# Reciprocal roots of head sums: spread to channel rows through DRAM instead of through TensorE

## The chip, the cores and the metric

The kernel runs on one core of one Trainium2 chip. The metric is the device time of one execution in microseconds (us); the median over the runs counts. One more execution of the same program was recorded by the hardware profiler, and its trace gives the rows that are quoted.

Engines are called as in the profile: PE is TensorE's matrix multiply, PEld its weight load, DVE is VectorE, ACT is ScalarE, POOL is GpSimd, SP is SyncE. "L681" is line 681 of the kernel before. A name with q (SPq) is an engine's DMA-issuing part.

## The reference

One layer of a hybrid model: a bidirectional RWKV-7 branch and a neighbourhood-attention branch over 640 tokens (512 latent ones and 128 of context), model width 1024, then a feed-forward block. The change lies in the RWKV branch, which has 8 heads of 64 channels. Two places of it matter: the L2 norm of `kk` per token and head, and the group norm of the recurrence's output `y` per token and head.

```python
kk = _heads(k * k_k).astype(jnp.float32)
kk = kk * lax.rsqrt(jnp.sum(kk * kk, axis=-1, keepdims=True) + L2_EPS)      # L2_EPS = 1e-12
...
s_f, y_f = _wkv_scan(s0[:, 0], ..., -kk, kk * iclr_fwd, False)
s_b, y_b = _wkv_scan(s0[:, 1], ..., -kk, kk * iclr_bwd, True)
y = y_f + y_b
mean = jnp.mean(y, axis=-1, keepdims=True)
var = jnp.mean(jnp.square(y - mean), axis=-1, keepdims=True)
y = (y - mean) * lax.rsqrt(var + GN_EPS) * ln_g + ln_b                      # GN_EPS = 64e-5
...
out = (y + bonus) * gate
```

In both, a sum over a head's 64 channels gives one number for each token and head, and its reciprocal root multiplies those 64 channels again.

## The kernel before, in words

**Layout.** Activations are kept with channels on the 128 partitions ("rows") and the 640 tokens along the free axis. The 512 channels of the branch make four tiles, `ct` = 0 to 3; a tile holds two heads, rows 0 to 63 and 64 to 127. Multiplying by a number per token and head therefore needs that number in 64 rows at once.

**Stages.** In the recurrence (from about 258 to 640 us of the span) each `ct` goes through four pieces of code:

- `main` and `inv`: the chunked form of the recurrence, with the inverse of triangular matrices. `inv` runs its rows s = 1 to 30 on DVE, transposes the outcome on DVE (L1345), and PE goes on with the first matmuls on it (L1358). Beside it runs `out` of the tile before (in `weave(inv, (og, bg))`, `og` is `out(ct-1)`, and `bg` the bonus term).
- `carry`: eight steps over the chunks of 64 tokens, of three yields each. A step is a chain PE (L1419), ACT (L1422), PE (L1448), ACT (L1454), PE (L1461), DVE (L1473), and the next step's L1419 waits for L1473. Beside it runs `prep` of the next tile (`pg`).
- `prep`: elementwise work that makes the next tile's operands. Its first part, `prep_a`, squares the keys (ACT, L662), sums each head by five small matmuls into a 128 x 10 tile, tokens on rows, (token block, head) in the columns (L666), adds 1e-12 and evacuates it (DVE, L670), and takes the power -1/2 (POOL, L671): `rk`. Then come the matmuls and tanh of a low-rank term (`lora`), and then `rk` is spread: ACT copies each of its columns 64 times along the free axis (L676), five PE transposes turn that into channel rows in PSUM (L681), and DVE multiplies the keys by it into `kk` (L684, L686: 512 and 128 columns, which lie in two PSUM tiles). After that come, for each direction d, a scaling (L695), a scan (L698) and two exponentials (L704, L709), and `prep_b`, which uses `kk`.
- `out`: group norm, gate and store of a tile. `inv_sqrt_bcast` does the same as above (L1130 matmuls, L1134, L1136 power, L1139 copy, L1144 transposes); L1497 and L1498 on DVE multiply by it, then come an affine step on ACT (L1499), L1501 and the gate.

**What sets the order.** PE, POOL, DVE and ACT run the recurrence in program order, which is laid out by hand (`tc.manual_schedule(engines=FIRST)`). SP, which issues most loads and stores, is placed by the framework's own scheduler. The pieces are Python generators. `weave` steps one of them and, at each yield, takes from the written plan `PRM["plan"]` how many projection matmuls (`fill`, L225) to put there, and how many steps of the others. Beside `inv` an entry counts yields of `out`. Beside `carry` an entry chooses a budget: `prep` yields its (ACT, DVE) cost in us, and `beside` steps it until the budget, (1.8, 0.8) or (1.3, 1.8), is used. `later` puts off the postprocessing of projections by some yields. `wload`/`wcast` at L176 to L197 load projection weights by SP, cast them on ACT (L192, L194) and make the low part by DVE or by a DMA that POOL issues (L193).

**Order around the change.** `prep` of ct 0 runs before the recurrence, with `prep` of ct 1, 2 and 3 beside the carries of ct 0, 1 and 2; `out` of ct 0, 1 and 2 runs beside the inversions of ct 1, 2 and 3, and that of ct 3 at the end. Buffers: `pre` (four buffers, 640 columns), `r10` (two, the 128 x 10 factors), PSUM `w` (six).

Of the kernel before, what the change touches and what calls it, by code (L numbers as in the profile page):

```python
# [14 lines left out]
P = 128  # L15
NT = 640
# [100 lines left out]
def body(ctx: ExitStack, tc: tile.TileContext, xs, xp, cols, consts, w_ada, b_row, w_rw, w_qkv,  # L117
# [26 lines left out]
    def nm(s):  # L144
        cn[0] += 1
        return f"{s}_{cn[0]}"
# [351 lines left out]
    def pre_t():  # L498
        return kp.tile([P, 643], F32, tag="pre", bufs=4, name=nm("pre"))[:, :NT]
# [131 lines left out]
    def parts(ct, k):  # L631

        return ((0, 320), (320, NT)) if ct and PRM[k] else ((0, NT),)

    def prep_a(ct, S, tpps, mid=None):

        S.Dt = kp.tile([P, 2, 10], F32, tag="Dt", bufs=2, name=nm("Dt"))
        S.P65 = [None, None]
        S.pre = []
        S.BK = []  # L640

        def lora(d, tw, ta):
            for (wi, bias, dst) in ((0, dcol(dhw0, 4 * d + ct), tw), (1, dcol(dha0, 4 * d + ct), ta)):
                for hf in range(2):
                    ps = tpps()
                    x = LX[wi][d]
                    pe.matmul(ps[:, :H2], S.uh[:, 2 * wi + d, :], x[:, hf * H2:(hf + 1) * H2],
                              start=True, stop=False)
                    pe.matmul(ps[:, :H2], S.ul[:, d, wi, :], x[:, hf * H2:(hf + 1) * H2],
                              start=False, stop=True)  # L650
                    if d == 0:
                        act.activation(dst[:, hf * H2:(hf + 1) * H2], ps[:, :H2], AF.Tanh,
                                       bias=bias, scale=0.5)
                    else:
                        act.activation(dst[:, (1 - hf) * H2:(2 - hf) * H2],
                                       V(ps[:, :], [[-1, H2]], H2 - 1), AF.Tanh,
                                       bias=bias, scale=0.5)
                    yield 0.45, 0

        sqt = pre_t()  # L660
        for (a, b) in parts(ct, "pa"):
            act.activation(sqt[:, a:b], kt_[:, a:b], AF.Square, scale=col("kk", ct))  # L662
        yield 2, 0
        ps = tpps()
        for i in range(5):
            pe.matmul(ps[:, 2 * i:2 * i + 2], sqt[:, i * 128:(i + 1) * 128], kc("blk2", 2),  # L666
                      start=True, stop=True)
        yield 0, 0
        rk = kp.tile([P, 10], F32, tag="r10", bufs=2, name=nm("r10"))
        dve.tensor_scalar(out=rk, in0=ps[:, :10], scalar1=1.0, scalar2=1e-12, op0=ALU.mult, op1=ALU.add)  # L670
        pool.tensor_tensor(out=rk, in0=rk, in1=mhalf[:, :10], op=ALU.pow)  # L671
        S.pre.append((pre_t(), pre_t()))
        yield 0, 0.2
        yield from lora(0, *S.pre[0])
        for (a, b) in parts(ct, "pa"):
            act.copy(V(sqt, [[64, (b - a) // 64], [1, 64]], a), V(rk[:, :], [[1, (b - a) // 64], [0, 64]], a // 64))  # L676
        yield 2, 0
        pa, pb = tpps(), tpps()
        for i in range(5):
            o_ = pa[:, i * 128:(i + 1) * 128] if i < 4 else pb[:, :128]  # L680
            pe.transpose(o_, sqt[:, i * 128:(i + 1) * 128], ident)  # L681
        yield 0, 0
        S.kk = kk = kk_t()
        dve.scalar_tensor_tensor(out=kk[:, :512], in0=kt_[:, :512], scalar=col("kk", ct),  # L684
                                 in1=pa[:, :512], op0=ALU.mult, op1=ALU.mult)
        dve.scalar_tensor_tensor(out=kk[:, 512:], in0=kt_[:, 512:], scalar=col("kk", ct),  # L686
                                 in1=pb[:, :128], op0=ALU.mult, op1=ALU.mult)
        yield 0, 1.2
        for d in range(2):
            if d:  # L690
                S.pre.append((pre_t(), pre_t()))
                yield from lora(1, *S.pre[1])

            tw = S.pre[d][0]
            dve.tensor_scalar(out=tw, in0=tw, scalar1=0.5, scalar2=0.5, op0=ALU.mult, op1=ALU.add)  # L695
            yield 0, 0.5
            for (a, b) in parts(ct, "pd"):
                dve.tensor_tensor_scan(tw[:, a:b], K[:, KO["scan"] + a:KO["scan"] + b], tw[:, a:b], 0.0,  # L698
                                       op0=ALU.mult, op1=ALU.add)
                yield 0, 1.6 * (b - a) / 640  # L700
            S.P65[d] = P65 = p65_t()
            pool.memset(P65[:, :, 0:1], 1.0)
            for (a, b) in parts(ct, "pa"):
                act.activation(P65[:, a // 64:b // 64, 1:65], V(tw, [[64, (b - a) // 64], [1, 64]], a), AF.Exp,  # L704
                               scale=-DEC_C)
                yield 0.9 * (b - a) / 640, 0
            act.copy(S.Dt[:, d, :], P65[:, :, 64])
            for (a, b) in parts(ct, "pa"):
                act.activation(tw[:, a:b], tw[:, a:b], AF.Exp, scale=DEC_C)  # L709
                yield 0.9 * (b - a) / 640, 0  # L710
            if mid and not d:
                yield from mid()

# [385 lines left out]
    with ExitStack() as s3:  # L1099
# [23 lines left out]
        def wps():  # L1123
            return pp.tile([P, 512], F32, tag="w", bufs=6, name=nm("w"))

        def inv_sqrt_bcast(sqt, scale, eps, ps_):

            ps = ps_()
            for i in range(5):
                pe.matmul(ps[:, 2 * i:2 * i + 2], sqt[:, i * 128:(i + 1) * 128], kc("blk2", 2),  # L1130
                          start=True, stop=True)
            yield
            r = kp.tile([P, 10], F32, tag="r10", bufs=2, name=nm("r10"))
            dve.tensor_scalar(out=r, in0=ps[:, :10], scalar1=scale, scalar2=eps, op0=ALU.mult,  # L1134
                              op1=ALU.add)
            pool.tensor_tensor(out=r, in0=r, in1=mhalf[:, :10], op=ALU.pow)  # L1136
            yield
            yield
            act.copy(c64(sqt), V(r[:, :], [[1, 10], [0, 64]]))  # L1139
            yield  # L1140
            pa, pb = ps_(), ps_()
            for i in range(5):
                o = pa[:, i * 128:(i + 1) * 128] if i < 4 else pb[:, :128]
                pe.transpose(o, sqt[:, i * 128:(i + 1) * 128], ident)  # L1144
            yield
            return pa, pb
# [337 lines left out]
        def out(ct, S):  # L1484

            y = S.y
            yc = out_t()
            ysq = pre_t()
            for hf in range(2):
                ps = wps()  # L1490
                hs_ = slice(hf * H2, (hf + 1) * H2)
                pe.matmul(ps[:, :H2], kc("blkj", 128), y[:, hs_], start=True, stop=True)
                act.copy(yc[:, hs_], ps[:, :H2])
                act.activation(ysq[:, hs_], ps[:, :H2], AF.Square)
                yield
            pa, pb = yield from inv_sqrt_bcast(ysq, 1.0 / 64, 64e-5, wps)
            dve.tensor_tensor(out=yc[:, :512], in0=yc[:, :512], in1=pa[:, :512], op=ALU.mult)  # L1497
            dve.tensor_tensor(out=yc[:, 512:], in0=yc[:, 512:], in1=pb[:, :128], op=ALU.mult)  # L1498
            act.activation(yc, yc, AF.Identity, scale=col("lg", ct), bias=col("lb", ct))  # L1499
            yield  # L1500
            dve.tensor_tensor(out=yc, in0=yc, in1=S.bv, op=ALU.add)  # L1501
            yield
            for hf in range(2):
                hs_ = slice(hf * H2, (hf + 1) * H2)
                ps = wps()
                pe.matmul(ps[:, :H2], S.gup, lg_[:, hs_], start=True, stop=True)
                yield
                dve.tensor_tensor(out=yc[:, hs_], in0=ps[:, :H2], in1=yc[:, hs_], op=ALU.mult)
                if not hf:
                    if ct < 3:  # L1510
                        yo = kp.tile([P, 643], F32R, tag="pre", bufs=4, name=nm("yo"))[:, :NT], yc
                    else:
                        o3.extend(kp.tile([P, NT], F32R, tag=t, bufs=1, name=nm("o3")) for t in ("kt", "rt"))
                        yo = o3
                split(yo[0][:, hs_], yo[1][:, hs_], yc[:, hs_], eng_of(PRM["yo"][ct]))
                yield
            if ct < 3:
                stores.extend((o_d[i][4 + ct], t) for i, t in enumerate((yo[0].bitcast(F32), yc)))
                if ct == 2:
                    while stores:  # L1520
                        sp.dma_start(*stores.pop(0))
            if ct == 2:
                if o:
                    o_load(6, 7)
                marks.add("O2")
# [874 lines left out]
```

## Time and profile before

| | |
|---|---|
| median of 3 runs | 1136.23 us (1135.29 to 1136.40) |
| profiled execution | 1135.23 us |
| its span | 1133.1 us |
| granted PE clock, mean | 0.997 |
| instructions | 27124 |
| busy: PE, PEld, DVE, ACT, POOL | 97%, 86%, 72%, 50%, 22% |
| DMA | 179.05 MB, mean 158 GB/s |

The span is from the first to the last recorded work of the profiled execution, so the execution's own time is a little longer. Busy shares are means over a span of unlike stages. A group's row gives line, engine, operation, output <- input, shape and count, then busy time or min/median/max of one in ns. A timeline row gives the start, the duration in us, engine, line, operation, operands; in brackets stands the idle time ahead of it and what ended that. A windows row gives, for a stretch in us, its length, each engine's busy us and its instruction count, the granted clock, the DMA engines' busy share and GB/s.

### The profile page before, as it was taken

The numbers are of one execution on the slowest core, as the hardware profiler recorded it, in microseconds if no ns is written. First come the engines' busy times: TensorE is split into PE (matmuls) and PEld (weight loads), VectorE is DVE, ScalarE is ACT, GpSimd is POOL, SyncE is SP. The second block draws the span as 40 slices with busy tenths as digits, with TensorE's granted clock in tenths as the row PEclk, the third lists the DMA queues.
The fourth block names the chain that finished last, engine by engine and source line by source line (L and its number), as shares of the span: only waits on it lengthen the run. The fifth ranks groups of instructions, "written<-read, shape, count | busy, mean of one in ns | idle before, by whom it ended". The sixth has DMA issues, their size and how long they took to land. (4 is left out here: it accounts for less than half of the span.)

```text
span 1133.1 us, 27124 instructions
## 1 busy us (share of the span) xinstructions
PE 1098.5 (97%) x11118; PEld 971.1 (86%) x11118; DVE 814.1 (72%) x1709; ACT 571.8 (50%) x1106; POOL 245.7 (22%) x318
## 2 busy tenths in 40 slices
PE   6999999999999999999899999999999999999998
PEld 4688878789888988888898788998999989989987
DVE  4565465669648937946787846899788887889854
ACT  4444566665566575467443534564453543444430
POOL 1163234321101111210100431151212122131100
PEclk9999999999999999999999999999999999999999
DMA  9753677644423453353743873477567567665622
GB/s 340 270 105 103 186 263 264 209 140 120 123 60 93 109 140 88 95 134 78 262 129 107 256 226 121 139 179 185 139 176 181 145 157 178 173 169 143 157 85 93
DMA packets 72995, 179.05 MB, mean 158 GB/s; under 512 B 8708, under 2 KB 23684, under 8 KB 72872
## 3 DMA queue, kind: packets, MB, share of 16 engines
q1 hardware_dynamic: 58488, 140.86, 37.8%
q0 software_dynamic: 12368, 33.56, 16.2%
q10 hardware_dynamic: 2016, 2.90, 0.8%
q8 instruction: 87, 1.43, 0.5%
q14 instruction: 36, 0.29, 0.1%
HBM read 137.81 MB, written 16.94 MB: 137 GB/s over the span
## 5 line engine op out<-in xcount | busy, mean ns | idle before, releaser
L1929 PE MATMUL f<-t,whi 128*128 128x320 f32 x640 | 141.8, 309 | 0.8 <-ACT whi L1974 0.5
L1929 PE MATMUL f<-b,whi 128*128 128x320 f32 x608 | 135.1, 310 | 0.4 <-DVE b L214 0.4
L225 PE MATMUL fl<-h,whi 128*128 128x320 f32 x672 | 121.1, 320 | 0.1
L1929 PEld LDWEIGHTS f<-t,whi 128*128 128x128 f32 x640 | 106.8, 188 | 1.4 <-ACT whi L1974 0.7
L225 PEld LDWEIGHTS fl<-h,whi 128*128 128x128 f32 x672 | 101.4, 188 | 4.9 <-issue 0.2
L1929 PEld LDWEIGHTS f<-b,whi 128*128 128x128 f32 x608 | 101.8, 188 | 1.2 <-issue 0.6
L1929 PE MATMUL f<-t,wlo 128*128 128x320 f32 x320 | 99.0, 309 | 0.2 <-DVE wlo L1977 0.2
L1929 PE MATMUL f<-b,wlo 128*128 128x320 f32 x304 | 94.0, 309 | 0.1
L194 ACT CAST whi<-wst 128x1024 fp32r<-128x1024 f32 (+1 forms) x67 | 69.0, 1031 | 38.6 <-PE acc L313 27.3
L313 PE MATMUL acc<-whi,h 128*128 128x512 f32 x240 | 78.5, 401 | 0.6 <-DVE h L438 0.6
L1974 ACT CAST whi<-ws 128x1024 fp32r<-128x1024 f32 x40 | 42.1, 1052 | 68.9 <-PE f L1929 42.2
L193 POOL DMA_DIRECT2D wlo<-wst x28 | 24.9, 888 | 192.6 <-ACT wlo L192 176.4
L197 DVE TENSOR_TENSOR wlo<-wst,whi 128x1024 fp32r<-128x1024 f32 (+2 forms) x47 | 48.1, 1033 | 25.7 <-ACT whi L194 25.5
L225 PE MATMUL fl<-h,wlo 128*128 128x320 f32 x336 | 62.7, 317 | 0.0
L1929 PEld LDWEIGHTS f<-t,wlo 128*128 128x128 f32 x320 | 60.1, 188 | 0.5 <-DVE wlo L1977 0.5
L1473 DVE TENSOR_TENSOR ZV<-w,Dt 64x128 f32<-64x128 f32 x64 | 18.4, 288 | 54.5 <-PE w L1461 53.3
L1929 PEld LDWEIGHTS f<-b,wlo 128*128 128x128 f32 x304 | 57.1, 188 | 0.4 <-DVE wlo L1977 0.4
L1988 POOL TENSOR_TENSOR ws<-wst 128x512 f32<-128x512 f32 x20 | 30.8, 1542 | 121.0 <-DVE wlo L1977 81.5
L1977 DVE TENSOR_TENSOR wlo<-ws,whi 128x1024 fp32r<-128x1024 f32 x40 | 53.7, 1342 | 4.1 <-ACT whi L1974 4.1
L313 PEld LDWEIGHTS acc<-whi,h 128*128 128x128 f32 x240 | 44.8, 188 | 12.5 <-issue 2.2
L225 PEld LDWEIGHTS fl<-h,wlo 128*128 128x128 f32 x336 | 51.2, 188 | 1.9
L984 POOL TENSOR_TENSOR L<-L,m 128x384 f32<-128x384 f32 (+1 forms) x40 | 32.1, 824 | 94.0 <-DVE m L983 75.1
(379 smaller groups left out, 2826.4 us busy)
## 6 DMA issues: line engine op xcount, KB each, us to landing
wst<-in_w_dram SPq DMA_DIRECT2D x58, 512.0 KB
wst<-in_w_rw_dram SPq DMA_DIRECT2D x31, 512.0 KB
wlo<-wst POOLq DMA_DIRECT2D x28, 512.0 KB, 4.8
wa<-in_w_ada_dram SPq DMA_DIRECT2D x24, 512.0 KB
f<-in_w_ada_dram SPq DMA_DIRECT2D x16, 512.0 KB
t<-in_w_dram SPq DMA_DIRECT2D x16, 512.0 KB
wst<-in_w_qkv_dram SPq DMA_DIRECT2D x12, 512.0 KB
o<-o_d SPq DMA_DIRECT2D x14, 320.0 KB
```

The costliest lines, as they stand in the source:

```text
L193: pool.dma_start(lo[:, :n].bitcast(F32), st[:, :n], accum_op=ALU.add)
L194: act.copy(hi[:, :n], st[:, :n])
L197: dve.tensor_tensor(out=lo[:, a:b], in0=st[:, a:b], in1=hi[:, a:b].bitcast(F32), op=ALU.subtract)
L225: pe.matmul(ps[:, :t1 - t0], w[:, a:a + 128], x[:, k0 + kt, t0:t1], start=n == 0, stop=n == 3 * nk - 1)
L313: pe.matmul(pss[i][:, a:b], lhs(x, kt, ts_), w[:, cs_], start=ki == 0 and n == 0, stop=ki == last and n == 2)
L984: pool.tensor_tensor(out=L, in0=L, in1=V(m[:, :], [[0, w]], 3), op=ALU.mult)
L1473: dve.tensor_tensor(out=V(ZV[own, l + 1, h, :], [[128 * dl, 2], [1, 64]]), in0=V(pn[own, :], [[64, 2], [1, 64]], 64 * g), in1=V(Dt[own, 0, ...
L1929: pe.matmul(ps[:, :H2], w_[:, c_], x_[:, kt, :], start=first and kt + n == 0, stop=last and kt == 3 and n == 2, skip_group_check=more)
L1974: act.copy(r[0][:, :width], src())
L1977: dve.tensor_tensor(out=r[1][:, :width], in0=src(), in1=r[0][:, :width].bitcast(F32), op=ALU.subtract)
L1988: eng_x(PRM["se"][i - 1]).tensor_tensor(out=o_, in0=x, in1=y, op=op)
```

## The change

`spread(r, t)` is new. It takes a 128 x 10 tile of factors and fills a 128 x 640 SBUF tile with them on channel rows, by three DMAs that POOL issues: one writes `r` transposed into a DRAM scratch of 10 x 128 (a column's 128 values become a row of 512 B), and one for each head reads five rows of it into 64 partitions at once.

In `prep` of ct 1, 2 and 3 it stands right behind the power, in place of the copy and the transposes, and the target is `sqt`, the tile of the squares. `kk` becomes one DVE operation on all 640 columns, reads `sqt` in SBUF, and stands behind the exponentials of d = 0. What the generator yields for the copy, (2, 0), stays; (0, 0) and (0, 1.2) go; (0, 0.8) comes behind the new `kk`. In `out` of ct 0 and 1 (`far`) it stands right behind the power as well, with the target `ysq`; as many yields as before follow, and one DVE product of 640 columns from SBUF replaces the two from PSUM. `prep` of ct 0 and `out` of ct 2 and 3 keep the transposes.

```diff
+    def spread(r, t):
+        r_d = dp.tile([10, P], F32, name=nm("r_d"))
+        pool.dma_start(r_d.rearrange("c p -> p c"), r)
+        for h in range(2):
+            x = r_d[h]
+            pool.dma_start(V(t[hrows[h], :], [[128, 5], [1, 128]]),
+                           bass.AP(x.tensor, x.offset, [[0, 64], [256, 5], [1, 128]]))
...
         pool.tensor_tensor(out=rk, in0=rk, in1=mhalf[:, :10], op=ALU.pow)
+        if ct:
+            spread(rk, sqt)
         S.pre.append((pre_t(), pre_t()))
         yield 0, 0.2
         yield from lora(0, *S.pre[0])
...
         S.kk = kk = kk_t()
+        if ct:
+            yield 2, 0
+        else:
...
+            yield 0, 1.2
...
                 act.activation(tw[:, a:b], tw[:, a:b], AF.Exp, scale=DEC_C)
                 yield 0.9 * (b - a) / 640, 0
+            if ct and not d:
+                dve.scalar_tensor_tensor(out=kk, in0=kt_, scalar=col("kk", ct), in1=sqt, op0=ALU.mult, op1=ALU.mult)
+                yield 0, 0.8
...
-        def inv_sqrt_bcast(sqt, scale, eps, ps_):
+        def inv_sqrt_bcast(sqt, scale, eps, ps_, far):
...
             pool.tensor_tensor(out=r, in0=r, in1=mhalf[:, :10], op=ALU.pow)
+            if far:
+                spread(r, sqt)
+                for _ in range(4):
+                    yield
+                return None, None
             yield
             yield
             act.copy(c64(sqt), V(r[:, :], [[1, 10], [0, 64]]))
...
-            pa, pb = yield from inv_sqrt_bcast(ysq, 1.0 / 64, 64e-5, wps)
-            dve.tensor_tensor(out=yc[:, :512], in0=yc[:, :512], in1=pa[:, :512], op=ALU.mult)
-            dve.tensor_tensor(out=yc[:, 512:], in0=yc[:, 512:], in1=pb[:, :128], op=ALU.mult)
+            pa, pb = yield from inv_sqrt_bcast(ysq, 1.0 / 64, 64e-5, wps, ct < 2)
+            if ct < 2:
+                dve.tensor_tensor(out=yc, in0=yc, in1=ysq, op=ALU.mult)
+            else:
+                dve.tensor_tensor(out=yc[:, :512], in0=yc[:, :512], in1=pa[:, :512], op=ALU.mult)
+                dve.tensor_tensor(out=yc[:, 512:], in0=yc[:, 512:], in1=pb[:, :128], op=ALU.mult)
```

More of the change, by code (lines that the diff above doesn't have):

```diff
@@ L674, in prep_a @@
         yield from lora(0, *S.pre[0])
[L675 to L682, printed above, removed]
-        S.kk = kk = kk_t()
[L684 to L688, printed above, removed]
+        S.kk = kk = kk_t()
+        if ct:
+            yield 2, 0
+        else:
+            act.copy(c64(sqt), V(rk[:, :], [[1, 10], [0, 64]]))
+            yield 2, 0
+            pa, pb = tpps(), tpps()
+            for i in range(5):
+                o_ = pa[:, i * 128:(i + 1) * 128] if i < 4 else pb[:, :128]
+                pe.transpose(o_, sqt[:, i * 128:(i + 1) * 128], ident)
+            yield 0, 0
+            for (a, b, p_) in ((0, 512, pa), (512, NT, pb)):
+                dve.scalar_tensor_tensor(out=kk[:, a:b], in0=kt_[:, a:b], scalar=col("kk", ct),
+                                         in1=p_[:, :b - a], op0=ALU.mult, op1=ALU.mult)
+            yield 0, 1.2
         for d in range(2):
```

## The prediction

> **What bounds the kernel now.** I read the page's busy shares first, then cut the recurrence into its stages with the view of windows, and then read each engine's timeline where the change sits.
>
> ```profile
> PE 1098.5 (97%) x11118; PEld 971.1 (86%) x11118; DVE 814.1 (72%) x1709; ACT 571.8 (50%) x1106; POOL 245.7 (22%) x318
> ```
>
> PE is busy 97% of the span, so as a rule a microsecond counts only if PE loses it or is made to wait for it. Each row below is a stage, with busy us of PE, PEld, DVE, ACT and POOL: the inversions of ct 1 and ct 2 first (with `out` of ct 0 and ct 1 beside them), then the carries of ct 0, 1 and 2 (with `prep` of ct 1, 2 and 3).
>
> ```profile
> 348.00:386.04 38.04, 36.60 (x768) 34.03 (x750) 34.22 (x134) 20.57 (x41) 7.89 (x18) 1.00 0.35 95
> 441.00:480.71 39.71, 36.69 (x688) 33.91 (x687) 34.03 (x132) 21.36 (x41) 8.25 (x16) 1.00 0.36 98
> 296.90:349.00 52.10, 48.89 (x754) 42.35 (x753) 26.79 (x47) 31.56 (x78) 7.64 (x13) 0.97 0.39 103
> 394.30:441.00 46.70, 45.57 (x754) 39.83 (x754) 26.48 (x46) 31.23 (x79) 10.12 (x14) 1.00 0.45 114
> 489.00:540.00 51.00, 49.91 (x807) 43.91 (x806) 25.17 (x45) 33.18 (x84) 7.62 (x13) 1.00 0.44 112
> ```
>
> In the carries PE is full and DVE half idle: what PE is spared there is gained. In the inversions DVE is nearly as full as PE (34 of 38 and of 40 us), and the stage ends in a meeting of the two: DVE's transpose (L1345) feeds PE's first matmul after it (L1358).
>
> ```profile
> 383.83 2.06 DVE L1345 STREAM_TRANSPOSE f<-RL 128x1024 f32<-128x1024 f32 x1
> 386.04 1.47 PE L1358 MATMUL w<-f,Nt 32*32 32x32 f32 x80 [0.36 <-DVE f L1345]
> 477.65 2.07 DVE L1345 STREAM_TRANSPOSE f<-RL 128x1024 f32<-128x1024 f32 x1
> 480.71 1.47 PE L1358 MATMUL w<-f,Nt 32*32 32x32 f32 x80
> ```
>
> In ct 1 PE has already waited 0.36 us for DVE: any DVE delay in that stage lengthens it one for one, and PE work saved in it is lost in that wait. In ct 2 DVE is done at 477.65 + 2.07 = 479.72 and PE comes 0.99 us later: a delay up to that is free.
>
> **The change, part by part.** The new path runs five times: `prep` of ct 1, 2, 3, and `out` of ct 0, 1.
>
> *Removed on PE:* five transposes each time. In the carry they take from 313.00 to the next instruction at 313.63.
>
> ```profile
> 313.00 0.71 PE L681 MATMUL w<-K,pre 128*128 128x128 f32 x5
> 313.63 0.45 PE L1419 MATMUL w<-ZV,AG 128*64 128x64 f32 x8
> ```
>
> So 0.63 us each. What follows in the carry (L1419) waits for nothing there, so the three `prep` calls give up to 3 x 0.63 = 1.89 us; in the ct 2 inversion up to 0.63; in ct 1, nothing.
>
> *Removed on ACT, swapped on DVE:*
>
> ```profile
> L676 ACT COPY pre<-r x7: 449/459/717, 200.7 to 502.4; 128x320 f32<-128x320 f32 x6, 128x640 f32<-128x640 f32 x1
> L1497 DVE TENSOR_TENSOR out<-out,w x4: 673/678/689, 369.1 to 631.3; 128x512 f32<-128x512 f32 x4
> L1498 DVE TENSOR_TENSOR out<-out,w x4: 272/278/281, 369.7 to 631.9; 128x128 f32<-128x128 f32 x4
> L1501 DVE TENSOR_TENSOR out<-out,bv x4: 805/820/826, 371.4 to 633.2; 128x640 f32<-128x640 f32 x4
> L1153 DVE SCALAR_TENSOR_TENSOR bv<-bv,D,rt__625 x4: 875/883/884, 260.0 to 545.2; 128x640 f32<-128x640 f32 x4
> ```
>
> ACT loses two copies of 0.46 us in `prep` and one of all 640 columns in `out`, 0.72 by the longest of this row; it is two thirds busy at most, so I count nothing. In `out`, 0.678 + 0.278 becomes one pass over SBUF like L1501, 0.82: DVE gains 0.14. In `prep` `kk` becomes one pass like L1153, 0.88, and goes behind the exponentials of d = 0, where DVE is half idle.
>
> *Added on POOL: three transfers.* The write W puts neighbouring values of `rk` 512 B apart, so it is 128 x 10 = 1280 runs of 4 B; each read R has 64 x 5 = 320 runs of 512 B, and the first read must wait on POOL until W has landed.
>
> ```profile
> q0 software_dynamic: 12368, 33.56, 16.2%
> 741.64 2.47 POOL L2077 DMA_DIRECT2D t<-in_w_dram  x2
> 953.34 1.78 POOL L2077 DMA_DIRECT2D t<-in_w_dram  x2
> DMA to landing us min/median/max: 3.7/5.9/11.8
> ```
>
> The packets of q0, POOL's queue, fit one packet for each contiguous run: 77 transfers of 128 runs, ten of which have 256, and 16 more packets for each transfer make 9856 + 1280 + 1232 = 12368. The pair at 741.64 has 256 runs each (it reads each half row twice), the pair at 953.34 has 128: 128 more runs cost (2.47 - 1.78) / 2 = 0.345 us. One of 128 takes about 0.87. W is then 0.87 + 9 x 0.345 = 4.0 us on POOL (at least 0.87, if runs that small cost nothing more); the two reads, with 64 runs more than the 256 pair, 2.47 + 0.34 = 2.8 us (at least 1.78).
>
> From the end of the issue to the landing:
>
> ```profile
> 312.95 0.35 SPq L1469 DMA_DIRECT2D out_dram<-zf  x1
> 313.80:314.00 0.20, 0.20 (x12) 0.20 (x12) 0.20 (x1) 0.00 (x0) 0.00 (x0) 1.00 0.84 251
> 314.00:314.20 0.20, 0.20 (x14) 0.20 (x11) 0.20 (x1) 0.07 (x1) 0.00 (x0) 1.00 0.28 74
> 314.20:314.40 0.20, 0.20 (x13) 0.20 (x8) 0.20 (x2) 0.20 (x1) 0.00 (x0) 1.00 0.00 0
> ```
>
> A 64 KB store ends its issue at 313.30, and the DMA engines are quiet from 314.2 (the last two columns of the rows are their share and GB/s): 0.9 us at least. The shortest landing on POOL's queue above, 3.7 us less 0.86 of issue, gives 2.84 at most, for 256 KB. I take 1.2, near the lower end, since 5 and 164 KB move here. From the end of the power to the broadcast in SBUF that makes T = 4.0 + 1.2 + 2.8 + 1.2 = 9.2 us, with ends at 0.87 + 0.9 + 1.78 + 0.9 = 4.45 and 4.0 + 2.84 + 2.8 + 2.84 = 12.5.
>
> *Who waits in the inversions.*
>
> ```profile
> 359.77 1.98 POOL L1136 TENSOR_TENSOR r<-r,mhalf 128x10 f32<-128x10 f32 x1 [5.99 <-DVE r L1134]
> 369.07 0.68 DVE L1497 TENSOR_TENSOR out<-out,w 128x512 f32<-128x512 f32 x1
> 454.39 2.08 POOL L1136 TENSOR_TENSOR r<-r,mhalf 128x10 f32<-128x10 f32 x1 [7.58 <-DVE r L1134]
> 462.89 0.67 DVE L1497 TENSOR_TENSOR out<-out,w 128x512 f32<-128x512 f32 x1
> ```
>
> `out` has as many yields as before, so DVE reaches the product at the same place among the rows of the inversion, and the whole inversion queues behind it. In ct 1 the spread starts at 361.75 and DVE is there at 369.07: a stall of T - 7.32, less the 0.14 saved, all of it passed on: T - 7.46 = +1.74. In ct 2 it starts at 456.47 against 462.89: T - 6.42 - 0.14, less the 0.99 us by which PE came late: +1.65 (at best -0.63).
>
> *Who waits in the carries.*
>
> ```profile
> 305.56 1.98 POOL L671 TENSOR_TENSOR r<-r,mhalf 128x10 f32<-128x10 f32 x1 [1.92 <-DVE r L670]
> 322.60 0.61 DVE L1473 TENSOR_TENSOR ZV<-w,Dt 64x128 f32<-64x128 f32 x2 [5.18 <-PE w L1461]
> 401.17 1.98 POOL L671 TENSOR_TENSOR r<-r,mhalf 128x10 f32<-128x10 f32 x1
> 416.30 0.61 DVE L1473 TENSOR_TENSOR ZV<-w,Dt 64x128 f32<-64x128 f32 x2 [0.84 <-PE w L1461]
> 500.00 1.98 POOL L671 TENSOR_TENSOR r<-r,mhalf 128x10 f32<-128x10 f32 x1 [3.36 <-DVE r L670]
> 510.27 0.61 DVE L1473 TENSOR_TENSOR ZV<-w,Dt 64x128 f32<-64x128 f32 x2 [0.47 <-PE w L1461]
> 512.12 0.45 PE L1419 MATMUL w<-ZV,AG 128*64 128x64 f32 x8
> ```
>
> Behind `kk` on DVE stands the next state update L1473, and PE's L1419 waits for that. By the costs that the generator yields and the budgets of `beside`, `kk` falls just before these L1473. For ct 1 and 2 `kk` ends at 307.54 + 9.2 + 0.88 = 317.6 and 403.15 + 10.1 = 413.2, well before 322.60 and 416.30: nothing waits, and each gains 0.63. For ct 3 it ends at 501.98 + 10.1 = 512.1, L1473 at 512.7, and L1419 slips from 512.12: about T - 8.6 = +0.6 in place of -0.63.
>
> *What queues behind the three transfers on POOL.*
>
> ```profile
> 367.43 0.92 POOL L193 DMA_DIRECT2D wlo<-wst  x1 [5.59 <-ACT wlo L192]
> DMA to landing us min/median/max: 4.4/4.8/9.3
> 372.39 0.33 SPq L176 DMA_DIRECT2D wst<-in_w_rw_dram  x1
> 377.81 1.04 ACT L192 ACTIVATE wlo<-wst 128x1024 fp32r<-128x1024 f32 x1
> ```
>
> POOL is free at 361.75 + 8.0 = 369.75, so this weight's low part goes out 2.3 us late; it lands 4.4 us on, and SP's next weight load, which waits for the buffer, moves from 372.39 to about 374.7. The cast at 377.81 still leaves it 3.1 us. If the load takes the 4.4 us of a transfer of its size, the cast is 1.3 us late, inside the 1.74 by which DVE has already moved that stage. I count nothing; without that cover it would be 1.3 us. The zeroing of `U` and of `P65`'s first column also move back, and nothing near needs them.
>
> *Sum.* 1.74 + 1.65 - 0.63 - 0.63 + 0.6 = +2.7 us. As a function of T it is 3T - 24.9 (even at T = 8.3), never below -0.14 - 4 x 0.63 = -2.7. The profiled execution took 1135.23 us (span 1133.1, 2.1 around it), so 1138.0; the median of the runs, 1136.23, lies 1.0 higher, so the forecast for the median is 1139.0.
>
> **The rivals.**
> *Faster: small runs cost next to nothing.* With an issue that doesn't grow with the runs, T is near the lower end of 4.45 us, every product finds its factors ready, and the kernel takes 1136.23 - 2.7 = 1133.5. For it: POOL spends hardly more on 256 runs than on 128. Against: the 0.345 us is there in every pair of that kind, and W has ten times as many runs. It decides below T = 7.3. The Trainium skill ("DMA: Bandwidth & Descriptors", section on the anatomy of one DMA) says that many descriptors can be emitted before the incremental cost shows; by that rule this rival would hold, and the pairs above, which show a cost at 256 already, speak against it.
>
> *No measurable change: T between 7.3 and 9.05.* The stalls eat the saved PE time; around 1136. For it: my T is a sum of four estimates, and 0.15 us less already lands here.
>
> *Much slower: 4-byte writes are slow in the DMA engines.* The store above is 128 runs of 512 B, and kept 16 engines busy for 0.84 and 0.28 of two slices of 0.2 us: (0.84 + 0.28) x 0.2 x 16 / 128 = 28 ns a packet, by my estimate. If each 4 B write had to read as well, 2 x 28 ns x 80 packets per engine = 4.5 us come on W, T = 13.7 at most, and the sum is 3 x 13.7 - 24.9 = +16: 1152. Nothing on the page shows a write this small. The Trainium skill (same page, Specifications) says that below 512 B the engine does a read-modify-write; by that rule this rival's price would apply. No run here shows it.
>
> **How the numbers follow.** About 0.2%, 2.3 us, is what a measurement of this kernel can tell from no change: T under 7.3 is faster, over 9.05 slower. Chances: faster rival 0.22, no change 0.28, slower 0.50, of which 0.38 with T to 11.5 (own range 1138.5 to 1146) and 0.12 for slow writes. The range, 1133 to 1146, goes from the faster rival (with half a us to spare) to T = 11.5 (+9.6) and leaves out the slow writes.
>
> **What would show it.** W's issue on POOL: 4 us right, under 1.5 wrong. The wait on POOL between W and the first read: about 1.2; over 4 means slow writes. DVE's product in `out` idle before it, released by a DMA, 1.9 and 2.8 us; no wait there makes the forecast wrong. L1358 in ct 1 idle by over 2 us instead of 0.36. L1473 in the carry of ct 2 late behind `kk`. L1419 after the place of L681 earlier by 0.63 in the carries of ct 0 and 1. A forecast with these right and another total would be wrong in what passes a stall on.

## The result: the changed kernel is 4.3% slower

The changed kernel takes 1184.61 us (median of four runs, 1182.13 to 1186.47), the kernel before 1135.76 us beside it. The ratio is 1.0428, with a 95% interval of 1.0408 to 1.0448: 49 us more, where 2.7 were forecast. The profiled execution took 1186.47 us.

The page of the changed kernel, its span and busy shares:

```profile
span 1184.5 us, 27089 instructions
PE 1107.9 (94%) x11093; PEld 979.5 (83%) x11093; DVE 813.4 (69%) x1704; ACT 568.5 (48%) x1098; POOL 258.9 (22%) x333
```

PE has 25 matmuls fewer than before and is yet 9.4 us longer busy, so its matmuls became slower; the rest, 42 us, is PE standing still. The view of windows of the changed kernel, cut at the same matmuls as the prediction's stages (carry 0, inversion 1, carry 1, inversion 2, carry 2):

```profile
295.33:356.09 60.76, 51.77 (x689) 44.76 (x692) 25.67 (x45) 31.08 (x75) 9.43 (x15) 0.89 0.36 93
356.09:402.87 46.78, 38.62 (x763) 35.45 (x745) 34.13 (x133) 19.93 (x40) 10.38 (x21) 0.89 0.32 84
411.19:466.77 55.58, 47.95 (x748) 41.86 (x747) 26.12 (x45) 30.55 (x77) 12.60 (x17) 0.91 0.43 102
466.77:516.51 49.74, 38.13 (x682) 35.25 (x681) 33.67 (x131) 20.73 (x40) 10.69 (x19) 0.90 0.32 83
524.84:589.57 64.73, 52.12 (x803) 45.66 (x803) 25.75 (x45) 32.66 (x82) 10.49 (x16) 0.89 0.44 94
```

Every one of the five stages with a spread is longer, by 9.7, 8.7, 8.9, 10.0 and 13.5 us from matmul to matmul, 51 together, and in each the granted clock is 0.89 to 0.91, where it was 0.97 to 1.00 before. So look at the spread itself. POOL's timeline in `out` of ct 0, and in `prep` of ct 3 (L638 is W, L641 the two reads):

```profile
367.53 1.99 POOL L1151 TENSOR_TENSOR r<-r,mhalf 128x10 f32<-128x10 f32 x1 [5.66 <-DVE r L1149]
369.82 1.05 POOL L638 DMA_DIRECT2D r_d<-r  x1 [0.30 <-POOL r L1151]
381.77 1.39 POOL L641 DMA_DIRECT2D pre<-r_d  x2 [10.90 <-DMA r_d<-r]
...
538.11 1.05 POOL L638 DMA_DIRECT2D r_d<-r  x1 [0.30 <-POOL r L680]
552.93 1.38 POOL L641 DMA_DIRECT2D pre<-r_d  x2 [13.78 <-DMA r_d<-r]
```

W costs POOL 1.05 us and not 4.0, and then the first read waits 10.90 and 13.78 us for W to land, where 1.2 was put. The other three waits are 12.14, 9.55 and 9.87 us; for two of them the view names a PE event as the one that came last. DVE waits for the reads in `out` (L1518) and for `kk` (L724):

```profile
385.96 0.82 DVE L1518 TENSOR_TENSOR out<-out,pre 128x640 f32<-128x640 f32 x1 [9.13 <-DMA pre<-r_d]
498.81 0.83 DVE L1518 TENSOR_TENSOR out<-out,pre 128x640 f32<-128x640 f32 x1 [10.26 <-DMA pre<-r_d]
323.77 0.89 DVE L724 SCALAR_TENSOR_TENSOR kk<-kt__626,C,pre 128x640 f32<-128x640 f32 x1 [4.46 <-DMA pre<-r_d]
438.07 0.89 DVE L724 SCALAR_TENSOR_TENSOR kk<-kt__626,C,pre 128x640 f32<-128x640 f32 x1 [7.71 <-DMA pre<-r_d]
557.12 0.88 DVE L724 SCALAR_TENSOR_TENSOR kk<-kt__626,C,pre 128x640 f32<-128x640 f32 x1 [14.53 <-DMA pre<-r_d]
```

T, from the end of the power to the start of the product, is 17.9, 16.4, 18.1, 16.6 and 19.3 us in order of time, against 9.2 in the prediction. Who stands behind DVE is told by the view of waits from 296 to 400 us (waiter <- releaser, us, times, longest):

```profile
ACT out L1522 <- DVE out L1518: 11.6, 1, 11.6
PE fl L225 <- ACT U L542: 7.2, 1, 7.2
ACT pre L664 <- DVE kk L724: 4.5, 1, 4.5
PE w L1468 <- ACT x L1442: 4.0, 2, 3.8
```

In `out` of ct 0, ACT's affine step waits for the product, and behind it on ACT waits the copy L542, which evacuates a projection's PSUM tile that PE wants. In carry 0, ACT's tanh L664 waits for `kk`, and behind it the carry's copy L1442. In these two stages PE stops through ACT's queue, which the prediction had not followed. In the other three it stops for DVE's own queue, as the prediction had it: in the inversion of ct 2 for 8.50 us at L1235, and in carries 1 and 2 for the state update behind `kk` (L1493, L1473 before), by PE's timeline:

```profile
441.25 0.91 PE L1439 MATMUL w<-ZV,AG 128*64 128x64 f32 x7 [5.82 <-DVE ZV L1493]
558.38 0.91 PE L1439 MATMUL w<-ZV,AG 128*64 128x64 f32 x7 [10.95 <-DVE ZV L1493]
```

### The profile page after: what moved, and what is told of

The parts are those of the page before. It is cut to its first block, busy times and chain, and to the rows that moved or that the text cites. A ratio compares the mean times of both kernels' runs of the same rounds, so it can differ in the third digit from the quotient of the medians.

```text
span 1184.5 us, 27089 instructions
## 1 busy us (share of the span) xinstructions
PE 1107.9 (94%) x11093; PEld 979.5 (83%) x11093; DVE 813.4 (69%) x1704; ACT 568.5 (48%) x1098; POOL 258.9 (22%) x333
## 3 DMA queue, kind: packets, MB, share of 16 engines
q1 hardware_dynamic: 58488, 140.86, 36.6%
q0 software_dynamic: 13248, 35.22, 16.4%
## 4 chain that ended last, share of the span: by engine, by line
PE 36%; issue 6%; DVE 5%; DMA 3%; ACT 2%; POOL 1%; DVEq 0%; POOLq 0%; ACTq 0%
PE f L1952 20%; PE acc L313 7%; PE y L2213 4%; PE fl L225 2%; DMA wlo<-wst 1%; DMA wlo<-t 1%; DVE wlo L2000 1%; DMA t<-in_w_dram 1%; PE fl L589 1%; PE fl L1737 1%; DVE hq L1840 1%; DVE wlo L2126 0%; ACT wlo L192 0%; DVE Y L2247 0%; DMA pre<-r_d 0%
## 5 line engine op out<-in xcount | busy, mean ns | idle before, releaser
L225 PE MATMUL fl<-h,whi 128*128 128x320 f32 x672 | 124.8, 327 | 7.2 <-ACT U L542 7.2
L225 PEld LDWEIGHTS fl<-h,whi 128*128 128x128 f32 x672 | 104.6, 194 | 12.5 <-ACT U L542 7.4
L1493 DVE TENSOR_TENSOR ZV<-w,Dt 64x128 f32<-64x128 f32 x64 | 18.5, 288 | 67.8 <-PE w L1481 57.1
L225 PE MATMUL fl<-h,wlo 128*128 128x320 f32 x336 | 64.1, 323 | 0.0
L225 PEld LDWEIGHTS fl<-h,wlo 128*128 128x128 f32 x336 | 52.7, 193 | 2.0
```

Of the source, the lines that this page charges most:

```text
L225: pe.matmul(ps[:, :t1 - t0], w[:, a:a + 128], x[:, k0 + kt, t0:t1], start=n == 0, stop=n == 3 * nk - 1)
L1493: dve.tensor_tensor(out=V(ZV[own, l + 1, h, :], [[128 * dl, 2], [1, 64]]), in0=V(pn[own, :], [[64, 2], [1, 64]], 64 * g), in1=V(Dt[own, 0, ...
```

## Experiments

**Longer runs in W.** One edit in the changed kernel:

```diff
-        pool.dma_start(r_d.rearrange("c p -> p c"), r)
+        pool.dma_start(bass.AP(r_d.tensor, r_d.offset, [[10, P], [1, 10]]), r)
```

> The changed kernel with one edit: the write W lays the 5 KB into the scratch as they lie in SBUF, 128 runs of 40 B in place of 1280 runs of 4 B; bytes, queue, reads and order stay (the factors reach wrong rows, so this one is for its time only). Theory 1, single 4 B writes to DRAM are slow to complete: POOL's wait between W and the first read falls from 10 to 14 us to 2 to 3 us, T to about 8 us, and the time to 1133 to 1140 us. Theory 2, any write and read back through DRAM on POOL's queue takes that long: the wait stays near 10 us and the time above 1175 us.

Measured: 1136.90 us against 1136.87, ratio 1.0008 (0.9991 to 1.0025). Page, POOL's timeline and DVE's timeline of this run:

```profile
PE 1095.0 (97%) x11093; PEld 968.1 (85%) x11093; DVE 813.5 (72%) x1704; ACT 569.1 (50%) x1098; POOL 257.6 (23%) x333
...
361.38 0.64 POOL L638 DMA_DIRECT2D r_d<-r  x1 [0.30 <-POOL r L1151]
365.25 1.39 POOL L641 DMA_DIRECT2D pre<-r_d  x2 [3.23 <-ACT fl L575]
...
369.57 0.83 DVE L1518 TENSOR_TENSOR out<-out,pre 128x640 f32<-128x640 f32 x1 [1.18 <-DMA pre<-r_d]
463.90 0.83 DVE L1518 TENSOR_TENSOR out<-out,pre 128x640 f32<-128x640 f32 x1 [1.06 <-DMA pre<-r_d]
510.58 0.89 DVE L724 SCALAR_TENSOR_TENSOR kk<-kt__626,C,pre 128x640 f32<-128x640 f32 x1 [3.75 <-DMA pre<-r_d]
```

The whole loss is gone with the layout of 5 KB. The same 5120 bytes on the same queue, read back by the same reads, let POOL go on after 3.23 us (1.8 to 4.3 over the five). The trip through DRAM is not what costs; theory 2 falls. T is 9.2, 8.5, 9.8, 7.4 and 8.5 us. The first line also shows what the clock did: the same 11093 PE instructions are 12.9 us shorter busy than in the changed kernel.

**W alone, read by nobody.** The kernel before, with this behind each of the five powers:

```diff
+        r_d = dp.tile([10, P], F32, name=nm("r_d"))
+        pool.dma_start(r_d.rearrange("c p -> p c"), r)
```

> The kernel before, with W alone added behind the five powers; nothing reads the scratch, and the transposes stay. Theory 1a, the slow writes also hold the DMA engines, so that loads and instruction fetches stand behind them: 3 to 15 us slower than before, with packets of other queues that take over 2 us each right after a W. Theory 1b, only the completion is late and the engines are free: within 2 us of before. Theory 2: the same as 1b.

Measured: ratio 1.0093 (1.0060 to 1.0126), 10.6 us, as theory 1a has it. W's source view, and the view of DMA for 3.6 us in carry 1 with a weight load under way, of this run (first q1 line) and of the kernel before (second):

```profile
DMA to landing us min/median/max: 10.4/10.5/10.5
q1 hardware_dynamic: 21, 0.09, 117.5%
```
```profile
q1 hardware_dynamic: 288, 0.59, 55.0%
```

The share is packet time over 16 engines' time (a packet's time is counted in whole, so it can pass 100%). Before, 288 packets of SP's queue moved 0.59 MB; behind W 21 packets moved 0.09 MB and took 1.175 x 16 x 3.6 / 21 = 3.2 us each on average. So this load stood behind W, and an 8 KB packet of the instruction queue (q14) behind the W in carry 0 took 3.5 us in place of 0.55. Not every packet is slowed: in `out` of ct 0 the 144 packets of SP's store L576 took 0.05 us each behind W, as in the kernel before. But this store landed (the last update of its semaphore in the trace) 8.0 us after the end of its issue, in place of 1.5. Windows and ACT's timeline of the same run show where PE and ACT stood still:

```profile
415.00:417.00 2.00, 0.65 (x5) 0.38 (x3) 0.83 (x1) 0.00 (x0) 0.00 (x0) 1.00 2.09 33
417.00:419.00 2.00, 0.00 (x0) 0.00 (x0) 0.00 (x0) 0.04 (x1) 0.00 (x0) 1.00 0.02 10
...
319.28 0.54 ACT L1463 COPY ZV<-w 64x128 f32<-64x128 f32 x2 [5.28 <-remote]
418.96 0.54 ACT L1463 COPY ZV<-w 64x128 f32<-64x128 f32 x2 [4.56 <-remote]
```

In carries 0 and 1 ACT stops at a copy between PSUM and SBUF that has nothing to do with W, and goes on 11.1 and 10.4 us after W's start, about when W lands; the profile names no instruction of the core that released it. These two stages got 5.4 and 5.3 us longer, carry 2 1.3, the inversions nothing. The semaphore that ACT waited for is PE's: the trace has the update that belongs to L1457 here 5.2 and 4.5 us after L1457 ended, where the kernel before has it 0.03 us after the same matmul. What held that update back, no view shows, so it stays open. The Trainium skill ("DMA: Bandwidth & Descriptors", queues, rings and completion order) says that a transfer's semaphore increment lands only after every earlier write of that DMA engine, across its queues. The trace agrees: the packets of the store L576 had passed by 372.2, and its semaphore was updated from 378.9 us on, when the last update for W had come at 377.8.

**What makes a write late.** Four kernels, each the kernel before with a write and a tiny read of it behind each power; POOL's wait between the two is the time to landing. Each was executed once.

> The kernel before, with a pair added behind each of the five powers: a write of the factors, and a tiny read of it on POOL's queue, whose wait shows when the write has landed. In order of time: (1) W as in the change; (2) 128 runs of 40 B; (3) 4 B each, every value 64 B from the next; (4) W's pattern for 2 of the 10 columns, 256 values; (5) 896 values of 4 B, 8 B apart, into SBUF in place of DRAM. Theory 1: waits of about 10, 2 to 3, 10, 3 to 4 us, and (5) 2 to 3 us if DRAM is the slow part, about 8 if any 4 B write is. A variant of it, that neighbours in one 64 B stretch get in each other's way: (3) 2 to 3 us. Theory 2: about 10 us in (1) to (4).

> As the run before, with other writes. In order of time: (1) 1280 values of 4 B, 8 B apart, a token's ten values next to each other; (2) 896 values of 4 B into SBUF; (3) 128 runs of 40 B; (4) 4 B each, 64 B apart; (5) W as in the change, but issued by SP's hardware queue. Theory 1: about 10, the same as in the run before for (2) to (4), and 10 in (5). If POOL's own making of the descriptors is the slow part: (1) and (4) about 10, and (5) 2 to 3 us. Theory 2: about 10 us in (1), (3), (4) and (5).

> The kernel before, with a write and a tiny read behind each power, as in the two probes, all writes of 4 B values into DRAM on POOL's queue. In order of time: (1) 1280 values 32 B apart; (2) 1280 values 16 B apart; (3) 128 values 4 B apart (one column); (4) 256 values 64 B apart; (5) 640 values 4 B apart. If the wait goes by how many values share a stretch of 64 B: about 5, 6, 8, 2.5, 9 us. If it goes by the number of values: 10, 10, 2.5, 3, 6 us.

> The kernel before, with a write of 1280 single values into DRAM and a tiny read behind each power. In order of time: (1) a token's ten values next to each other, 16 B apart; (2) a column's values 8 B apart; (3) a token's ten values 8 B apart, as in an earlier probe (9.8 us there); (4) a column's values 12 B apart; (5) W as in the change. If it goes by the distance, and 16 B is enough: 3 to 5, 10, 10, 5 to 10, 10 us. If it goes by the order in which the values of a stretch are written: (1) also near 10 us, as (3), and (2) nearer to the 4 us of columns 16 B apart.

POOL's timeline of the first probe (W's pattern, 40 B runs, 64 B apart, two columns, SBUF), and the SP-issued W of the second:

```profile
321.11 0.56 POOL L644 DMA_DIRECT2D back<-r_d  x1 [10.21 <-DMA r_d<-r]
370.60 0.58 POOL L648 DMA_DIRECT2D back<-r_d  x1 [3.35 <-DMA r_d<-r]
413.40 0.57 POOL L656 DMA_DIRECT2D back<-r_d  x1 [4.38 <-DMA r_d<-r]
470.75 0.56 POOL L652 DMA_DIRECT2D back<-r_d  x1 [8.48 <-DMA r_d<-r]
511.21 0.56 POOL L664 DMA_DIRECT2D back<-rt__954_7004  x1 [2.51 <-DMA rt__954_7004<-r]
```
```profile
517.03 0.59 POOL L668 DMA_DIRECT2D back<-r_d  x1 [13.87 <-DMA r_d<-r]
```

| single 4 B values, to DRAM unless said | wait, us |
|---|---|
| columns, 4 B apart (W): 1280 / 640 / 256 / 128 values | 10.2, 12.2 / 10.3 / 8.5 / 7.5 |
| columns, 1280 values 8 / 12 / 16 / 32 / 64 B apart | 5.0 / 4.5 / 3.9 / 4.5 / 4.4, 4.5 |
| columns, 256 values 64 B apart | 3.1 |
| a token's ten values in a row, 8 / 16 B apart | 9.8, 8.6 / 7.3 |
| 128 runs of 40 B | 3.4, 2.2 |
| 896 values into SBUF, 8 B apart | 2.5, 2.4 |

Not mainly the number of values: 128 neighbours take longer than 1280 spaced ones, though fewer neighbours land somewhat sooner. Not POOL's queue: issued by SP, W's wait is as long (its issue ended at 504.4, so 12.7 us). Not small writes as such: into SBUF, or 64 B apart, they land soon. What is slow is single values into DRAM right beside each other. By distance alone it doesn't go either, since a token's ten values are still slow at 16 B where a column's are not; what decides is left open. A cell is one wait at one place in the kernel, and the same W waits 9.6 to 13.8 us in the change's five places, so differences of 2 us or so say little.

Of the expectations, theory 1 as first put, that any single 4 B write into DRAM is slow, missed at 64 B apart (4.4 us, not 10) and at two columns (8.5, not 3 to 4). In the third probe the number of values in one stretch of 64 B came out within about 2 us and the number of values in all didn't (4.5 and 3.9 us where 10 were due). Neither rule of the fourth came out: a token's values 16 B apart took 7.3 us, and a column's 8 B apart 5.0.

**Late factors without small writes.** In the 40 B kernel, six idle powers between W and the reads:

```diff
+        for _ in range(6):
+            junk = kp.tile([P, 10], F32, tag="junk", bufs=1, name=nm("junk"))
+            pool.tensor_tensor(out=junk, in0=r, in1=mhalf[:, :10], op=ALU.pow)
```

> The kernel with the 40 B write (factors reach wrong rows, for its time only), with six idle powers on POOL between the write and the reads, 12 us, so that the factors come as late as in the change (T = 0.3 + 0.64 + 12 + 1.4 + 3.3 = 17.6 us against 16.4 to 19.3) while no small write stands in the DMA engines. If the lateness is what costs: by the slacks of the prediction, 2 x (17.6 - 7.5) in the inversions, 17.6 - 8.6 in the carry of ct 2, 2.8 and 4.7 in those of ct 0 and 1, 37 us in all, and some more for the clock after each stall: 1172 to 1178 us, so that this and the 10.6 us of W alone make up the change's 49. If the held DMA engines are what costs: below 1150 us.

Measured: 1188.88 us, ratio 1.0469 (1.0455 to 1.0483). Timelines of POOL, DVE and ACT:

```profile
308.14 12.72 POOL L641 TENSOR_TENSOR junk<-r,mhalf 128x10 f32<-128x10 f32 x6
389.55 0.82 DVE L1521 TENSOR_TENSOR out<-out,pre 128x640 f32<-128x640 f32 x1 [12.15 <-DMA pre<-r_d]
560.90 0.89 DVE L727 SCALAR_TENSOR_TENSOR kk<-kt__626,C,pre 128x640 f32<-128x640 f32 x1 [12.49 <-DMA pre<-r_d]
325.79 0.53 ACT L667 ACTIVATE pre<-w,D 128x320 f32<-128x320 f32 x1 [8.90 <-DVE kk L727]
```

T is 17.6, 19.5, 17.8, 18.2 and 17.3 us, on average 18.1 against 17.7 in the change, and the loss is 53 us against 49. Lateness alone makes the whole loss. Of the transfers held by W little is seen beside it (in carry 0 of the change PE stands 2.2 us for ACT's L1474, which no instruction released); their 10 us probably lie under the same waits. My 37 us and some were too little for it, so the prediction's slacks were wrong too.

**The buffer behind ACT's wait.** `prep` takes five `pre` tiles out of four buffers, so the last tanh writes where the squares were, and that is the tile the reads fill. The same kernel, with the reads into another one:

```diff
-            spread(rk, sqt)
+            S.kk = kk = kk_t()
+            spread(rk, kk)
```

> The run with the six idle powers once more (factors reach wrong rows, for its time only), with one edit: in prep the reads go into the tile of kk itself, and no longer into the tile of the squares, which is one of the four pre buffers that the later low-rank tanh on ACT writes. If ACT's wait for that buffer is why the prediction's slack for the carries of ct 0 and 1 was too large: its wait for kk is gone, these two cost 2.8 and 4.9 us by the slacks of the prediction in place of 10.9 and 9.0, and the time falls by about 12 us to 1175 to 1180. If DVE's L1473 behind kk is the gate anyway: 1185 to 1190 us.

Measured: 1183.35 us, ratio 1.0417 (1.0392 to 1.0442), 6 us less than the run before by the ratios. DVE's and ACT's timelines in carry 0:

```profile
325.05 0.89 DVE L728 SCALAR_TENSOR_TENSOR kk<-kt__626,C,kk 128x640 f32<-128x640 f32 x1 [9.97 <-DMA kk<-r_d]
325.96 0.61 DVE L1497 TENSOR_TENSOR ZV<-w,Dt 64x128 f32<-64x128 f32 x2
327.35 0.27 ACT L1446 COPY x<-w 128x128 f32<-128x128 f32 x1 [5.99 <-PE w L1443]
```

ACT no longer waits for `kk`; the carry now waits for L1497 behind `kk` on DVE, the path of the prediction. Carry 0 is 4.4 us longer than before in place of 9.0, carry 1 7.4 in place of 8.7. So the buffer was real and worth 4.6 us in carry 0, 1.3 in carry 1, half of what I expected.

**A version without small writes.** `prep` alone, with one small transpose, rows of 512 B, and `kk` at the end of `prep_a`:

```diff
-        pool.dma_start(r_d.rearrange("c p -> p c"), r)
+        pool.dma_start(r_d, r)
...
+            pt = tpps()
+            pe.transpose(pt[0:10, :P], rk, ident)
+            s = sb.tile([P, 256], F32, tag="pr", bufs=1, name=nm("pr"))[0:10, 0:P]
+            act.copy(s, pt[0:10, :P])
+            spread(s, kk)
```

> A version that keeps what was gained and drops the small writes: in the three preps one PE transpose of the 128 x 10 factors and one ACT copy of 10 x 128, W as 10 rows of 512 B, the reads into the tile of kk itself, and kk made at the end of the first part of prep, so that T may be over 20 us; out keeps its transposes. If the sum's rows hold: 3 x (0.63 - 0.14) = 1.5 us faster than before, 1134 to 1136 us, which may be too little to tell. If a read that lands late or its place in the order costs: 1138 us or more.

Measured: 1133.75 us against 1135.82, ratio 0.9988 (0.9977 to 0.9999). The timelines of PE and POOL:

```profile
309.81 0.27 PE L687 MATMUL w<-K,r 128*10 128x128 f32 x1
310.97 0.60 POOL L638 DMA_DIRECT2D r_d<-pr  x1 [4.77 <-ACT pr L689]
312.87 1.41 POOL L641 DMA_DIRECT2D kk<-r_d  x2 [1.30 <-DMA r_d<-pr]
...
409.14 1.41 POOL L641 DMA_DIRECT2D kk<-r_d  x2 [4.06 <-DMA r_d<-pr]
505.51 1.40 POOL L641 DMA_DIRECT2D kk<-r_d  x2 [3.12 <-DMA r_d<-pr]
```

W lands 1.30, 4.06 and 3.12 us after its issue. The 0.12%, 1.4 us, is what three times 0.63 - 0.14 gives, but the interval only just leaves out no change, and the profiled execution doesn't place the gain: its three carries changed by -0.5, +0.6 and -0.6 us. This version is far ahead of the changed kernel; that it is ahead of the kernel before is likely and not shown.

## Why the prediction was wrong

- **The landing of W** is the step that failed: "I take 1.2, near the lower end, since 5 and 164 KB move here". It is 9.6 to 13.8 us. The row it came from is a store of 512 B runs, and its 0.9 is the time until the DMA engines fell quiet; what the change writes is single values beside each other in DRAM, which no row of before shows, and there the engines are quiet long before the landing (windows below). The upper bound of 2.84 came from loads into SBUF with runs of 1 KB and more, so it bounded nothing.
- **The much slower rival** had the right place (W's small writes) and a wrong size: 4.5 us on W by packets of 28 ns. The time is not in packets (no DMA engine has one from 378 to 380 us, in the windows below, while POOL waits until 381.77), but between them and the notice of the landing; and it gave T = 13.7 where 17.7 came. The Trainium skill ("DMA: Bandwidth & Descriptors", Specifications) has the rule that below 512 B the engine does a read-modify-write, by which the rival's price would apply; here 40 B runs landed in 1.8 to 4.3 us and 512 B rows in 1.3 to 4.1, so size below 512 B is not the condition. The Trainium skill (same page, anatomy of one DMA) says that the receipt of the write makes up most of a transfer's fixed time and can be surprisingly long into HBM. That fits the late W, though not why spaced values land soon, and the prediction did not use it.
- **W's issue**, 4.0 us, was 1.05: 1152 more runs cost 0.42 us over the 40 B form's 0.63. The fit of one packet per run did not hold: five spreads added 13248 - 12368 = 880 packets, 176 each, where 1280 + 2 x 320 runs were to come. W itself is 48 of them (W alone: 12608 - 12368 = 240 for five); issued by SP it is 59784 - 58488 = 1296 packets, 1280 and 16 more, and lands as late. The reads took 1.39 us to issue and, in the 40 B kernel, 2.6 to 3.9 to land, against 2.8 and 1.2. These misses cancel by luck: with 40 B runs T was 7.4 to 9.8, around the 9.2 predicted. There the sum's terms give -0.5 us, and the time was that of before.
- **3T - 24.9** gives 28 us for T = 17.7. With each stage's own T, and with the two carries that it treats as free past their slack (17.9 - 14.2 and 18.1 - 12.3), its terms are 3.7, 9.0, 5.8, 9.0 and 10.7 us in the order of the stages, 38 together, where 9.7, 8.7, 8.9, 10.0 and 13.5 were measured. So the inversions, which end when DVE is done, are right to 1 us, and 12 us are missing in the carries. Of these, ACT's wait for the `pre` buffer is 4.6 and 1.3 us, by the run that removes it. In carry 1 DVE has L707 and L710, 2.0 us, between `kk` and L1493, where the prediction put `kk` just before it. The rest, 1.4 us in carry 0 and 2.8 in carry 2, may be the clock (PE was 3.9 and 2.0 us longer busy there) and, in carry 0, the stop at L1474; no run takes either away alone. After a stall PE runs at half clock for some us; the windows of the changed kernel around the stall in `out` of ct 0:

```profile
378.00:380.00 2.00, 2.00 (x14) 1.84 (x13) 0.00 (x0) 0.00 (x0) 0.00 (x0) 1.00 0.00 0
...
382.00:384.00 2.00, 0.00 (x0) 0.00 (x0) 0.00 (x0) 0.00 (x0) 2.00 (x5) 0.71 0.25 88
...
388.00:390.00 2.00, 1.90 (x7) 1.90 (x8) 2.00 (x9) 0.05 (x1) 0.00 (x0) 0.50 0.50 139
390.00:392.00 2.00, 2.00 (x59) 1.67 (x60) 2.00 (x12) 0.46 (x1) 0.44 (x1) 0.50 0.46 164
392.00:394.00 2.00, 2.00 (x99) 1.87 (x97) 2.00 (x8) 1.12 (x4) 1.75 (x2) 0.73 0.00 0
```

  PE has 0.95 us of work left from 380 to 382, so it stops at about 380.9; by the 0.71 and 0.73 the clock falls at about 382.8 and is back at about 393.1, 5 us after PE is back at 388. Five such stalls, each with some 5 us of work at half clock, lose about 12.5 us, which fits the 12.9 us of longer matmuls. The Trainium skill ("TensorE: Matmul & The Clock Gate", part 1) says that an idle stretch of about 3.4 us halves the clock and as long a busy one restores it; the trace agrees in the halving, but here about 2 us idle were enough for it and the way back took 5.
- **Right**: the stalls in `out`, their place and, at the T that was foreseen, their size (in the 40 B kernel DVE idles 1.18 and 1.06 us before the product, where T - 7.32 and T - 6.42 are 1.17 and 0.97); the path through `kk` and DVE's state update; that POOL's late weight parts cost nothing seen at that T. PE's 0.63 us for each `prep` fits the totals, but the stages scatter as much. **Not as marked**: L1358 (now L1378) in ct 1 was to stand idle by over 2 us, and the changed kernel's PE timeline has

```profile
402.87 1.47 PE L1378 MATMUL w<-f,Nt 32*32 32x32 f32 x80 [0.27 <-DVE f L1365]
```

  because PE had lost its time earlier, at L225, through ACT's copy.

## What to carry to other kernels

A transpose hidden in the addresses of a DMA to DRAM was not free here, down to 512 B in all: write longer runs (40 B and 512 B landed soon here, and one small PE transpose buys the 512 B), and take a landing time only from a row with the same run length and the same target. A stall can cost more than its length, through whoever stands behind it on in-order queues and perhaps through the clock after it, so before making a value late, look for every buffer that its consumer holds.

## What was not expected of the hardware

- 128 single values, 512 B in all, written beside each other into DRAM take 7.5 us to land; 1280 of them 64 B apart take 4.4, and 5 KB in 40 B runs 1.8 to 4.3.
- While such a write was under way, packets of a weight load on another queue took 3.2 us each on average, and a copy on ACT that shares nothing with it stood still for 5 us. A store of another queue, whose packets were as fast as ever, landed 8.0 us after its issue in place of 1.5, behind the write.
